# Put-aways of begun products moved behind the second split in the first phase of a two-layer trunk; constants and most parameters loaded in the middle of it

## The chip, the cores and the metric

The kernel runs on one core of one Trainium2 chip. The metric is the device time of one execution in microseconds. The engines are TensorE (PE, matrix products), VectorE (DVE), ScalarE (ACT), GpSimd (POOL) and SyncE (SP, which issues the transfers). Each has a queue of its own that it works off in order; semaphores order the queues among each other.

## The reference, cut to what matters

The program computes two layers on 256 tokens of width 2048 in float32. Layer 0 is a Mamba-2 mixer, layer 1 an attention layer with dilated windows. This case touches the beginning of layer 0:

```python
mod = jax.nn.silu(c) @ w + b                       # per layer: shift, scale, gate
h = x * (1.0 + scale_c) + shift_c
proj = h @ in_w                                    # 2048 x 10304
z, xBC, dt = jnp.split(proj, [SSD_D_INNER, SSD_D_INNER + SSD_CONV_DIM], axis=-1)
xBC = jax.nn.silu(_causal_depthwise_conv(xBC, conv_w, conv_b))
...                                                # scan, gate z, norm, out_w
x = _layer_norm(DEEPNORM_ALPHA * x + (1.0 + gate_c) * y, ln_g[layer], ln_b[layer])
```

## The kernel before

**Products in three passes.** A float32 product is made from halves: `split` copies a raw weight piece (128x1024, 512 KB) to a rounded high half `whi` on ACT (line 93) and computes the low half `wlo` as the difference on DVE (line 95). TensorE then multiplies high by high, high by low and low by high. A *piece* holds two of the 16 tiles `kt` of the contraction (kt = 2q and 2q+1). `cm_piece` (lines 119 to 121) has the weights as the stationary operand and makes 24 matmuls of 256 columns for a piece; `tm_piece` with `tm_mults` (lines 173 to 175) has the activations as the stationary operand and makes 12 matmuls of 512 columns.

**The first phase.** The input `h` is not there at the start: its scale and shift come from `silu(c) @ ada_w`, which DVE computes in 32 dots over 1 MB of `araw` each (`ada_dot`, line 251), two for each kt. Once both dots of a kt are there, `h_step` adds the bias from `adab` (line 256), ACT makes `htmp` and the high half of h (lines 396, 397), and DVE the low half (line 398), which is held back in the list `late` and issued a little later. So kt after kt comes into being while the weights stream in, and TensorE has to work with the few kt that are there. For this the phase does not run one product after the other. Two products (`first`, items -2 and -1, "h" in the list) stay in four PSUM banks of their own for the whole phase. Ten more are *begun*: each takes the pieces whose kt exist already, its sums are then put away to SBUF (`place`), and the rest is added later. The order is written out by hand in `order`, in eight rows of seven pieces with two pieces of `dt` in the last; a dot after the name of a piece ends a stretch of that product. "b4:0." is piece 0 of product b4 and its end for now; "z4:1 z4:2." are pieces 1 and 2 of z4, and there it ends.

**Putting away.** When a stretch ends, the loop issues two instructions for the two PSUM tiles of the product: an ACT copy to `place` (line 486), or, where the product had been put away before, a DVE add (line 484). The other PSUM pool, `mm`, has four buffers, so that two products of the begun kind can be open.

**Transfers.** All loads are issued on SP's queue in program order. `fetch_piece` keeps six raw buffers, `fetch` four araw buffers; an issue waits until its buffer is free, and everything behind it on SP waits too. `prm` holds all small parameters (529 columns: the bias `adab` first with 96, then the convolution's weights and others), `cc` the constants (identity, triangle, mask; 512 columns). Both are loaded in the prologue between the first tiles of x and the first raw pieces.

**Order on an engine.** The program is traced in order, and a planner then sorts the instructions of each engine by its own estimates of when each becomes ready, with the traced order as the priority. `tc.issue_after(ins)` puts the instructions in its block behind `ins` on the queue of the engine of `ins`. The list `pin` holds such an instruction for the dots, `latest` the last low half that `split` issued.

**Behind the phase** come the convolutions of the first two products, the scan and the other products of layer 0, which add their last pieces to the begun sums, and then layer 1.

Of the kernel before, what the change touches and what calls it, by code (L numbers as in the profile page):

```python
# [9 lines left out]
F32 = mybir.dt.float32  # L10
F32R = mybir.dt.float32r
I32 = mybir.dt.int32
AF = mybir.ActivationFunctionType
ALU = mybir.AluOpType
# [4 lines left out]
P = 128  # L19
L = 256  # L20
D = 2048
KT = D // P
# [15 lines left out]
OFF, _o = {}, 0  # L38
# [3 lines left out]
NPAR = _o  # L42
# [7 lines left out]
def trunk(ctx, tc, xT, x, c, par, cst, bias, lnrow, ada, wdt, win, wout, wkv, wk1, wbin, wbout, out):  # L50
    nc = tc.nc
    V, S, T, PO = nc.vector, nc.scalar, nc.tensor, nc.gpsimd

    cons = ctx.enter_context(tc.tile_pool(name="cons", bufs=1))
# [11 lines left out]
    cb_ = cons.tile([P, D], F32, name="cb_")  # L66
    bcast(cb_, c)
    S.activation(cb_, cb_, AF.Silu)
    prm = cons.tile([P, NPAR], F32, name="prm")
    cc = cons.tile([P, NCONST], F32, name="cc")  # L70

    cons.tile([P, 32], F32, name="pad")

    def pv(name):
        a, b = OFF[name]
        return prm[:, a:b]

    ident = cc[:, CI:CI + 128]
    tri = cc[:, CT:CT + 128]
# [5 lines left out]
    def load_piece(src):  # L85
        raw = wp.tile([P, 1024], F32, name="raw", bufs=6)
        nc.sync.dma_start(raw, src)
        return raw

    def split(raw, into=None, after=None):  # L90

        hi, lo = into or [wp.tile([P, 1024], F32R, name=n, bufs=4) for n in ("whi", "wlo")]
        S.activation(hi, raw, AF.Copy)  # L93
        with tc.issue_after(after) if after is not None else ExitStack():
            latest[0] = V.tensor_tensor(lo, raw, hi.bitcast(F32), op=ALU.subtract)  # L95
        return hi.rearrange("p (k n) -> p k n", k=2), lo.rearrange("p (k n) -> p k n", k=2)

    jobs, latest, pin = [], [None], [None]

    def background(n, every=1):  # L100

# [4 lines left out]

    state = [0]

    def cm_piece(src, q, ps, ahi, alo, k0=0, k1=KT, raw=None, after=None):


        hi, lo = split(load_piece(src[q]) if raw is None else raw, after=after)
        for k in range(2):
            kt = 2 * q + k
            for n in range(4):
                o = ps[n // 2][:, n % 2, :]
                c_ = slice(n * P, n * P + P)
                first = kt == k0 and n % 2 == 0
                T.matmul(o, hi[:, k, c_], ahi[:, kt, :], start=first, stop=False, skip_group_check=True)  # L119
                T.matmul(o, hi[:, k, c_], alo[:, kt, :], start=False, stop=False, skip_group_check=True)  # L120
                T.matmul(o, lo[:, k, c_], ahi[:, kt, :], start=False, stop=kt == k1 - 1, skip_group_check=True)  # L121
# [37 lines left out]
    def tiles(ps):  # L159
        return [ps[n // 2][:, n % 2, :] for n in range(4)]  # L160

    def tm_piece(src, q, ps, ahi, alo, k0=0, k1=KT, raw=None):

        tm_mults(q, split(load_piece(src[q]) if raw is None else raw), ps, ahi, alo, k0, k1, range(2))

    def tm_mults(q, w, ps, ahi, alo, k0, k1, blocks, cols=slice(0, 512)):
        hi, lo = (t[:, :, cols] for t in w)
        for k in range(2):
            kt = 2 * q + k
            for b in blocks:  # L170
                h_, l_ = ahi(kt)[:, b * P:b * P + P], alo(kt)[:, b * P:b * P + P]
                o, part = ps[b][:, cols], cols != slice(0, 512)
                T.matmul(o, h_, hi[:, k, :], start=kt == k0, stop=False, skip_group_check=part)  # L173
                T.matmul(o, h_, lo[:, k, :], start=False, stop=False, skip_group_check=part)  # L174
                end = T.matmul(o, l_, hi[:, k, :], start=False, stop=kt == k1 - 1, skip_group_check=part)  # L175
        return end
# [54 lines left out]
    KIND = ("shift", "scale", "gate")  # L231
    mod = [cons.tile([P, KT, 3], F32, name=f"mod{i}") for i in range(2)]
    gated = [dr.tile([D], F32, name=f"gated{i}", bufs=1) for i in range(2)]
    adab = pv("adab").rearrange("p (i k j) -> p i k j", i=2, j=3)

    def shift(i, kt):
        return mod[i][:, kt, 0:1]
# [9 lines left out]
    def ada_dot(layer, kind, ct, raw):  # L247

        j = KIND.index(kind)
        with tc.issue_after(pin[0]) if pin[0] is not None else ExitStack():  # L250
            V.scalar_tensor_tensor(raw, raw, 1.0, cb_, op0=ALU.mult, op1=ALU.mult,  # L251
                                   accum_out=mod[layer][:, ct, j:j + 1])
# [32 lines left out]
    hhi, hlo = hp[:, 0], hp[:, 1]  # L285

    with ExitStack() as cA:
# [14 lines left out]
        with ExitStack() as cS:  # L302
# [21 lines left out]
            def bc_conv(g, t):  # L324
                for i in range(2):
                    bc[g + i] = p0.tile([P, 2, L], F32, name="bcm", bufs=3)
                    conv(t[2 * i], 32 + g + i, bc[g + i][:, 0, :])
                    conv(t[2 * i + 1], 40 + g + i, bc[g + i][:, 1, :])
# [37 lines left out]
            with ExitStack() as c0:  # L366
# [4 lines left out]
                raws, xts, late = [], {}, []  # L371

                def fetch():
                    i = len(raws)
                    if i < len(cols):
                        raws.append(ada_load((wp1, pe)[i // 2 % 2], *cols[i]))
# [5 lines left out]
                def h_step():  # L382

                    _, kind, kt = cols[h_step.i]
                    raw = raws[h_step.i]
                    h_step.i += 1
                    if kind == "scale" and kt % 2 == 0 and kt:
                        fetch_x(kt)
                    ada_dot(0, kind, kt, raw)
                    fetch()  # L390
                    while late:
                        late.pop()()
                    if kind == "shift":
                        ada_bias(0, slice(kt, kt + 1), slice(0, 2))
                        t = pe.tile([P, L], F32, name="htmp")
                        S.activation(t, xts[kt // 2][:, kt % 2, :], AF.Identity, bias=shift(0, kt), scale=scale(0, kt))
                        S.activation(hhi[:, kt, :], t, AF.Copy)
                        late.append(lambda: V.tensor_tensor(hlo[:, kt, :], t, hhi[:, kt, :].bitcast(F32),  # L398
                                                            op=ALU.subtract))
# [4 lines left out]
                part = {n: p[1:] for n, p in zip(names, begun.values())}  # L404
                two = "h"
                order = []
# [11 lines left out]
                source = {"dt": wdt, -2: win[0], -1: win[4], **{n: p[0] for n, p in zip(names, begun.values())}}  # L418
# [3 lines left out]
                def fetch_piece():  # L422
                    if len(pieces) < len(order):
                        k, q, _ = order[len(pieces)]
                        pieces.append(load_piece(source[k][q]))
# [1 line left out]
                fetch()  # L427
                fetch()
                fetch_x(0)
                nc.sync.dma_start(prm, par)  # L430
                nc.sync.dma_start(cc, cst)
                V.tensor_scalar(adab[:, :, :, 1:3], adab[:, :, :, 1:3], 1.0, None, op0=ALU.add)
                fetch_piece()
                fetch_piece()
# [2 lines left out]
                for _ in range(2):  # L437
                    for _ in range(2):
                        h_step()
                    while late:  # L440
                        late.pop()()
                    fetch_piece()

                def dt_piece(q, raw):
# [16 lines left out]
                        T.transpose(pt[:, 64 * b:64 * b + 64], row[:, b * P:b * P + P], ident[:64, :64])  # L461
                    V.tensor_copy(vv, pt)

                begin, done = {}, set()
                for i, (k, q, ends) in enumerate(order):
                    fetch_piece()
                    if k == "dt":
                        dt_piece(q, pieces[i])
                        continue
                    z = str(k)[0] == "z"  # L470
                    if k in part and k not in begin:
                        begin[k] = 2 * q
                        pss[k] = tm_pair() if z else acc_pair()
                    k0, k1 = (begin[k], 2 * q + 2 if ends else KT) if k in part else (0, KT)
                    if z:
                        tm_piece(source[k], q, pss[k], hh_, hl_, k0=k0, k1=k1, raw=pieces[i])
                    else:
                        cm_piece(source[k], q, pss[k], hhi, hlo, k0=k0, k1=k1, raw=pieces[i])
                    if ends:
                        del begin[k]  # L480
                        for w in range(2):
                            place = part[k][1][:, w, :] if z else part[k][1][:, 2 * w:2 * w + 2, :]
                            if k in done:
                                V.tensor_tensor(place, pss[k][w], place, op=ALU.add)
                            else:
                                S.activation(place, pss[k][w], AF.Copy)
                        done.add(k)

                    while h_step.i < min(len(cols), 4 + (i + 1) * 4 // 7):
                        h_step()  # L490
                    while late and h_step.i % 4 == 0:
                        late.pop()()
                bc_conv(0, tiles(first[0]))
                xs_conv(0, tiles(first[1]))
            aux = cS.enter_context(tc.tile_pool(name="aux", bufs=2, space=PSUM, reuse_waits="tile"))
# [533 lines left out]
```

## Time and profile before

| | us |
|---|---|
| median of 3 runs | 1297.56 |
| the runs | 1293.49 to 1298.24 |
| the profiled execution | 1296.34 |
| span in its profile, first to last instruction | 1294.5 |
| mean granted TensorE clock | 0.994 |

The span is cut by lines of the program: `L93` is line 93. A group names engine, operation, output and inputs, count, busy us, mean ns of one, and the idle time in front of its instructions with what ended it. A wait line reads "who waited <- for whom: us in total, times, longest". In a stretch, each engine has its busy time and, in brackets, its number of instructions. PE's ends are modelled, and a matmul counts as busy for longer than until the start of the next, so a PE that shows 10.0 us in 10 can still run at less than its pace. An instruction's idle time stands in square brackets at its end, with what released it.

### The profile page before, as it was taken

The page shows a single profiled execution, that of the slowest core. Times are in us where ns is not written, and L with a number is a line of the kernel's source. Part 1 is how long each engine was busy: PE and PEld are TensorE (multiplying, and loading weights), DVE is VectorE, ACT ScalarE, POOL GpSimd, SP SyncE. Part 2 cuts the span into 40 slices and gives each one's busy share as a digit, 9 for nine tenths or more (in the row PEclk, how much of TensorE's full clock was granted, in tenths as well). Part 3 has the DMA queues.
Part 4 walks back from the last instruction along what each step waited for, and adds up shares of the span by engine and source line. Part 5 has one row for each costly group of instructions (what it writes and reads, how often), then busy time and mean ns, then how long its engine had stood idle before and what let it go on. Part 6 is the DMA issues. An engine that isn't in the chain of part 4 may idle for free.

```text
span 1294.5 us, 19393 instructions
## 1 busy us (share of the span) xinstructions
PE 1247.4 (96%) x7414; PEld 1097.5 (85%) x7414; DVE 1027.1 (79%) x1453; ACT 707.7 (55%) x1033; POOL 27.5 (2%) x20
## 2 busy tenths in 40 slices
PE   4999999999999999999999799999999999999997
PEld 4879988899898999878888699888887888888885
DVE  6789887999999778899765577888777757758778
ACT  3545457867587687864333444444435644444651
POOL 0000000000000000000000043000000000000000
PEclk9999999999999999999999899999999999999999
DMA  9999967696884546398977575999897854363471
GB/s 382 422 398 419 374 210 243 219 342 248 290 313 170 183 161 212 128 338 326 385 258 218 190 238 170 338 393 365 329 342 275 275 187 155 98 187 107 147 276 65
DMA packets 80445, 335.86 MB, mean 259 GB/s; under 512 B 8960, under 2 KB 9056, under 8 KB 67552
## 3 DMA queue, kind: packets, MB, share of 16 engines
q1 hardware_dynamic: 80352, 334.62, 71.5%
q8 instruction: 58, 0.95, 0.3%
q14 instruction: 35, 0.29, 0.1%
HBM read 332.41 MB, written 2.18 MB: 258 GB/s over the span
## 4 chain that ended last, share of the span: by engine, by line
PE 81%; DVE 9%; DMA 5%; ACT 3%; issue 2%; SPq 0%; DVEq 0%; ACTq 0%
PE acc L151 12%; PE acc L174 11%; PE acc L175 11%; PE acc L173 11%; PE acc L121 8%; PE acc L119 8%; PE acc L120 8%; PE acc L152 6%; DMA araw<-in_ada 4%; DVE wlo L95 2%; DVE araw L251 2%; PE py L593 2%; PE aux L802 1%; ACT whi L93 1%; PE po L816 1%
## 5 line engine op out<-in xcount | busy, mean ns | idle before, releaser
L95 DVE TENSOR_TENSOR wlo<-raw,whi 128x1024 fp32r<-128x1024 f32 x395 | 484.4, 1239 | 188.5 <-ACT whi L93 187.5
L93 ACT ACTIVATE whi<-raw 128x1024 fp32r<-128x1024 f32 x395 | 413.0, 1056 | 334.3 <-PE acc L175 139.0
L119 PE MATMUL acc<-actT,whi 128*128 128x256 f32 x960 | 274.1, 289 | 23.2 <-ACT whi L93 19.3
L174 PE MATMUL acc<-wlo,actT 128*128 128x512 f32 x704 | 276.7, 393 | 3.2 <-DVE wlo L95 3.1
L121 PE MATMUL acc<-actT,wlo 128*128 128x256 f32 x960 | 270.8, 286 | 4.4 <-DVE wlo L95 4.4
L173 PE MATMUL acc<-whi,actT 128*128 128x512 f32 x704 | 272.2, 394 | 0.8 <-ACT actT L648 0.7
L120 PE MATMUL acc<-actT,whi 128*128 128x256 f32 x960 | 272.9, 286 | 0.0
L151 PE MATMUL acc<-actT,whi 128*128 128x512 f32 x704 | 251.6, 400 | 0.0
L251 DVE SCALAR_TENSOR_TENSOR araw<-araw,cb__72 128x2048 f32<-128x2048 f32 x96 | 219.3, 2286 | 17.9 <-DMA araw<-in_ada 17.5
L119 PEld LDWEIGHTS acc<-actT,whi 128*128 128x128 f32 x960 | 186.6, 196 | 25.1 <-ACT whi L93 20.3
L152 PE MATMUL acc<-actT,wlo 128*128 128x256 f32 x704 | 201.6, 286 | 0.1
L121 PEld LDWEIGHTS acc<-actT,wlo 128*128 128x128 f32 x960 | 184.6, 194 | 6.7 <-DVE wlo L95 6.4
L120 PEld LDWEIGHTS acc<-actT,whi 128*128 128x128 f32 x960 | 186.7, 194 | 0.4 <-DVE actT L398 0.2
L175 PE MATMUL acc<-whi,actT 128*128 128x512 f32 x448 | 175.0, 391 | 0.0
L174 PEld LDWEIGHTS acc<-wlo,actT 128*128 128x128 f32 x704 | 132.3, 188 | 33.5 <-DVE wlo L95 7.0
L151 PEld LDWEIGHTS acc<-actT,whi 128*128 128x128 f32 x704 | 132.4, 188 | 30.9
L173 PEld LDWEIGHTS acc<-whi,actT 128*128 128x128 f32 x704 | 131.8, 188 | 28.5 <-ACT actT L648 1.5
L152 PEld LDWEIGHTS acc<-actT,wlo 128*128 128x128 f32 x704 | 133.2, 189 | 0.8 <-DVE wlo L95 0.4
L175 PE MATMUL acc<-whi,ylo 128*128 128x512 f32 x256 | 100.3, 392 | 0.0
L175 PEld LDWEIGHTS acc<-whi,actT 128*128 128x128 f32 x448 | 84.1, 188 | 17.1
L175 PEld LDWEIGHTS acc<-whi,ylo 128*128 128x128 f32 x256 | 48.0, 188 | 9.5
L320 DVE SCALAR_TENSOR_TENSOR cacc<-acc,prm,cacc 128x253 f32<-128x253 f32 (+2 forms) x96 | 42.0, 474 | 5.5 <-ACT cacc L317 5.2
(212 smaller groups left out, 1093.0 us busy)
## 6 DMA issues: line engine op xcount, KB each, us to landing
araw<-in_ada SPq DMA_DIRECT2D x96, 1024.0 KB, 7.4
raw<-in_win SPq DMA_DIRECT2D x160, 512.0 KB, 5.3
raw<-in_wkv SPq DMA_DIRECT2D x72, 512.0 KB, 6.2
raw<-in_wout SPq DMA_DIRECT2D x64, 512.0 KB, 4.9
raw<-in_wbin SPq DMA_DIRECT2D x64, 512.0 KB, 4.3
raw<-in_wk SPq DMA_DIRECT2D x24, 512.0 KB, 8.6
cbc<-cumd SPq DMA_DIRECT2D x16, 512.0 KB, 5.4
raw<-in_wbout SPq DMA_DIRECT2D x16, 512.0 KB, 3.7
```

The lines of the kernel that those rows point to most:

```text
L93: S.activation(hi, raw, AF.Copy)
L95: latest[0] = V.tensor_tensor(lo, raw, hi.bitcast(F32), op=ALU.subtract)
L119: T.matmul(o, hi[:, k, c_], ahi[:, kt, :], start=first, stop=False, skip_group_check=True)
L120: T.matmul(o, hi[:, k, c_], alo[:, kt, :], start=False, stop=False, skip_group_check=True)
L121: T.matmul(o, lo[:, k, c_], ahi[:, kt, :], start=False, stop=kt == k1 - 1, skip_group_check=True)
L151: T.matmul(ps[n], hi[:, k, c_], xp[:, kt], start=kt == 0, stop=False, skip_group_check=True)
L152: T.matmul(ps[n][:, 0, :], lo[:, k, c_], xhi[:, kt, :], start=False, stop=kt == KT - 1, skip_group_check=True)
L173: T.matmul(o, h_, hi[:, k, :], start=kt == k0, stop=False, skip_group_check=part)
L174: T.matmul(o, h_, lo[:, k, :], start=False, stop=False, skip_group_check=part)
L175: end = T.matmul(o, l_, hi[:, k, :], start=False, stop=kt == k1 - 1, skip_group_check=part)
L251: V.scalar_tensor_tensor(raw, raw, 1.0, cb_, op0=ALU.mult, op1=ALU.mult, accum_out=mod[layer][:, ct, j:j + 1])
L320: V.scalar_tensor_tensor(acc[:, o:], ps[:, :L - o], w[:, j:j + 1], acc[:, o:], op0=ALU.mult, op1=ALU.add)
```

## The change

The change consists of four edits, all in the first phase.

1. `put_away` replaces the lines that put a begun product's sums away. A stretch that ends with piece i is noted in `ended`, and its put-away is traced in the next turn of the loop, behind the split of piece i+2: copies by `issue_after` behind that piece's ACT copy (`copied`), adds behind its low half (`latest`).
2. For that, each turn traces the split of its own piece (if that is not there yet) and of the next one ahead of the matmuls and of the dots. The pieces' functions get the halves (`w=halves[i]`) instead of the raw piece.
3. `adab` becomes a tile of its own, loaded in the prologue. The rest of `prm` is loaded in the loop at piece 16 and `cc` at piece 20.
4. In the prologue, `pin` is set to the low half of h, so that the dots of kt = 1 and the first of kt = 2 stand behind the low half before them; behind that dot the pin is taken away.

```diff
-    prm = cons.tile([P, NPAR], F32, name="prm")
+    NB = OFF["adab"][1]
+    adab_ = cons.tile([P, NB], F32, name="adab")
+    prm = cons.tile([P, NPAR - NB], F32, name="prm")
...
     def split(raw, into=None, after=None):
         hi, lo = into or [wp.tile([P, 1024], F32R, name=n, bufs=4) for n in ("whi", "wlo")]
-        S.activation(hi, raw, AF.Copy)
+        copied[0] = S.activation(hi, raw, AF.Copy)
...
                     ada_dot(0, kind, kt, raw)
+                    if kt > 1:
+                        pin[0] = None
                     fetch()
...
                 fetch_x(0)
-                nc.sync.dma_start(prm, par)
-                nc.sync.dma_start(cc, cst)
+                nc.sync.dma_start(adab_, par[:, :NB])
...
                     while late:
-                        late.pop()()
+                        pin[0] = late.pop()().ins
                     fetch_piece()
...
+                def put_away(k, ps, add):
+                    for w in range(2):
+                        place = part[k][1][:, w, :] if k[0] == "z" else part[k][1][:, 2 * w:2 * w + 2, :]
+                        with tc.issue_after((latest if add else copied)[0].ins):
+                            if add:
+                                V.tensor_tensor(place, ps[w], place, op=ALU.add)
+                            else:
+                                S.activation(place, ps[w], AF.Copy)
...
                 for i, (k, q, ends) in enumerate(order):
                     fetch_piece()
+                    if i == 16:
+                        nc.sync.dma_start(prm, par[:, NB:])
+                    if i == 20:
+                        nc.sync.dma_start(cc, cst)
+                    for j in (i, i + 1):
+                        if j < len(order) and j not in halves and order[j][0] != "dt":
+                            halves[j] = split(pieces[j])
+                    while ended:
+                        put_away(*ended.pop())
...
                     if ends:
                         del begin[k]
-                        for w in range(2):
-                            place = part[k][1][:, w, :] if z else part[k][1][:, 2 * w:2 * w + 2, :]
-                            if k in done:
-                                V.tensor_tensor(place, pss[k][w], place, op=ALU.add)
-                            else:
-                                S.activation(place, pss[k][w], AF.Copy)
+                        ended.append((k, pss[k], k in done))
                         done.add(k)
...
+                while ended:
+                    put_away(*ended.pop())
                 bc_conv(0, tiles(first[0]))
```

More of the change, by code (lines that the diff above doesn't have):

```diff
@@ L75, in pv @@
         a, b = OFF[name]
-        return prm[:, a:b]
+        return prm[:, a - NB:b - NB]
     ident = cc[:, CI:CI + 128]
@@ L96, in split @@
         return hi.rearrange("p (k n) -> p k n", k=2), lo.rearrange("p (k n) -> p k n", k=2)
-    jobs, latest, pin = [], [None], [None]
+    jobs, latest, copied, pin = [], [None], [None], [None]
     def background(n, every=1):
@@ L107, in trunk, with cm_piece @@
     state = [0]
-    def cm_piece(src, q, ps, ahi, alo, k0=0, k1=KT, raw=None, after=None):
-        hi, lo = split(load_piece(src[q]) if raw is None else raw, after=after)
+    def cm_piece(src, q, ps, ahi, alo, k0=0, k1=KT, w=None, after=None):
+        hi, lo = w or split(load_piece(src[q]), after=after)
         for k in range(2):
@@ L160, in tiles, with tm_piece @@
         return [ps[n // 2][:, n % 2, :] for n in range(4)]
-    def tm_piece(src, q, ps, ahi, alo, k0=0, k1=KT, raw=None):
-        tm_mults(q, split(load_piece(src[q]) if raw is None else raw), ps, ahi, alo, k0, k1, range(2))
+    def tm_piece(src, q, ps, ahi, alo, k0=0, k1=KT, w=None):
+        tm_mults(q, w or split(load_piece(src[q])), ps, ahi, alo, k0, k1, range(2))
     def tm_mults(q, w, ps, ahi, alo, k0, k1, blocks, cols=slice(0, 512)):
@@ L233, in trunk @@
     gated = [dr.tile([D], F32, name=f"gated{i}", bufs=1) for i in range(2)]
-    adab = pv("adab").rearrange("p (i k j) -> p i k j", i=2, j=3)
+    adab = adab_.rearrange("p (i k j) -> p i k j", i=2, j=3)
     def shift(i, kt):
@@ L462, in dt_piece @@
                     V.tensor_copy(vv, pt)
-                begin, done = {}, set()
+                def put_away(k, ps, add):
[6 more added lines that the diff above has]
+                                S.activation(place, ps[w], AF.Copy)
+                begin, done, ended, halves = {}, set(), [], {}
                 for i, (k, q, ends) in enumerate(order):
                     fetch_piece()
+                    if i == 16:
[7 more added lines that the diff above has]
+                        put_away(*ended.pop())
                     if k == "dt":
@@ L475, in trunk @@
                     if z:
-                        tm_piece(source[k], q, pss[k], hh_, hl_, k0=k0, k1=k1, raw=pieces[i])
+                        tm_piece(source[k], q, pss[k], hh_, hl_, k0=k0, k1=k1, w=halves[i])
                     else:
-                        cm_piece(source[k], q, pss[k], hhi, hlo, k0=k0, k1=k1, raw=pieces[i])
+                        cm_piece(source[k], q, pss[k], hhi, hlo, k0=k0, k1=k1, w=halves[i])
                     if ends:
                         del begin[k]
-                        for w in range(2):
-                            place = part[k][1][:, w, :] if z else part[k][1][:, 2 * w:2 * w + 2, :]
-                            if k in done:
-                                V.tensor_tensor(place, pss[k][w], place, op=ALU.add)
-                            else:
-                                S.activation(place, pss[k][w], AF.Copy)
+                        ended.append((k, pss[k], k in done))
                         done.add(k)
```

## The prediction

> **What bounds the kernel now.** First the page: which engine carries the span, and the price of the instructions that the change moves.
>
> ```profile
> span 1294.5 us, 19393 instructions
> ...
> PE 1247.4 (96%) x7414; PEld 1097.5 (85%) x7414; DVE 1027.1 (79%) x1453; ACT 707.7 (55%) x1033; POOL 27.5 (2%) x20
> ...
> L95 DVE TENSOR_TENSOR wlo<-raw,whi 128x1024 fp32r<-128x1024 f32 x395 | 484.4, 1239 | 188.5 <-ACT whi L93 187.5
> L93 ACT ACTIVATE whi<-raw 128x1024 fp32r<-128x1024 f32 x395 | 413.0, 1056 | 334.3 <-PE acc L175 139.0
> ```
>
> TensorE is busy 96% of the span, so the kernel gets faster only by what TensorE stands still, and the change reaches the first phase alone. Second, that phase in stretches (columns: busy us of PE, PEld, DVE, ACT, POOL with instruction counts, granted clock, DMA share, GB/s):
>
> ```profile
> 0.00:20.00 20.00, 4.14 (x17) 3.85 (x18) 9.58 (x12) 6.69 (x7) 0.20 (x4) 1.00 0.90 357
> 20.00:80.00 60.00, 54.58 (x327) 47.99 (x326) 49.10 (x53) 29.21 (x41) 0.00 (x0) 0.97 1.02 422
> 80.00:100.00 20.00, 18.16 (x101) 15.44 (x100) 17.39 (x20) 9.87 (x13) 0.00 (x0) 1.00 0.98 382
> 100.00:140.00 40.00, 40.00 (x279) 37.52 (x278) 34.78 (x37) 21.88 (x28) 0.00 (x0) 1.00 1.01 415
> 140.00:160.00 20.00, 18.34 (x151) 17.93 (x150) 18.90 (x21) 9.62 (x13) 0.00 (x0) 1.00 0.94 364
> 160.00:200.00 40.00, 38.27 (x245) 34.28 (x245) 33.78 (x53) 25.78 (x38) 0.00 (x0) 1.00 0.64 213
> ```
>
> TensorE idles in the start and, in lumps, at 20 to 100 and 140 to 200 us. The DMA engines are full (share 1.02, 422 GB/s) from 20 to 80 us and nearly so to 160: this decides below how much of a gain can stand. Third, the waits from 26 to 200 us, of PE, then of ACT, then of DVE (total us, times, longest):
>
> ```profile
> PE acc L119 <- ACT whi L93: 3.5, 3, 1.6
> PE acc L121 <- DVE wlo L95: 2.7, 5, 1.4
> PE acc L119 <- ACT actT L397: 2.3, 1, 2.3
> PE acc L174 <- DVE wlo L95: 2.1, 3, 1.4
> ...
> ACT y L486 <- PE acc L175: 19.0, 4, 6.4
> ACT sz L486 <- PE acc L175: 8.4, 2, 5.9
> ...
> ACT y L486 <- PE acc L121: 6.3, 4, 3.6
> ...
> ACT whi L93 <- DMA raw<-in_win: 0.2, 1, 0.2
> ...
> DVE y L484 <- PE acc L121: 5.1, 2, 2.8
> ```
>
> PE waits for splits: 3.5 + 2.7 + 2.1 = 8.3 us in 11 stops. ACT and DVE, which make the splits, stand in front of a put-away (L486, L484) until PE ends the product. Fourth, two places in order of time:
>
> ```profile
> 80.91 1.28 ACT L486 ACTIVATE sz<-acc 128x512 f32<-128x512 f32 x2 [5.86 <-PE acc L175]
> 82.08 2.00 ACT L93 ACTIVATE whi<-raw 128x1024 fp32r<-128x1024 f32 x2
> ...
> 83.19 0.39 PE L119 MATMUL acc<-actT,whi 128*128 128x256 f32 x1 [1.63 <-ACT whi L93]
> ...
> 139.61 0.69 DVE L484 TENSOR_TENSOR y<-acc,y 128x512 f32<-128x512 f32 x1 [2.77 <-PE acc L121]
> ...
> 140.94 1.22 DVE L95 TENSOR_TENSOR wlo<-raw,whi 128x1024 fp32r<-128x1024 f32 x1
> ...
> 142.21 0.38 PE L121 MATMUL acc<-actT,wlo 128*128 128x256 f32 x1 [1.44 <-DVE wlo L95]
> ```
>
> At 80.91 ACT has been idle for 5.86 us with a split queued behind the put-away; then come two copies, the split, and only then PE. At 139.61 the same on DVE. The stop has a fixed make-up: the put-away and a split follow the product's end while PE has at most one split piece left.
>
> **The change part by part.**
>
> *Put-aways behind the second split.* No instruction is added: 10 begun products still give 20 copies on ACT and 6 adds on DVE. When a product ends with piece i, ACT now holds the splits of i+1 and i+2 ahead of the copies, so PE has two pieces to eat (24 matmuls at a 0.12 us pitch, about 2.9 us each, 5.7 together) while ACT does 1.28 us of copies and one split of 1.06, and DVE one of 1.24. All 11 stops follow this pattern, so 8.3 us go. Each stop also costs refilling: a 128x512 matmul counts as busy for 0.39 us but the next starts 0.23 later, and the first starts after a stop come about 0.1 late; I take 0.26 per stop, 2.9 us in all (bounds 0 and 11 x 0.4 = 4.4). **Term: 11.2 us, bounds 8.3 and 12.7.**
>
> *What waits behind the put-away now.* On ACT the h pieces (L396, L397) and the split of i+3; these have the 5.7 us. PSUM buffers come free later by at most one split, 1.06 us; this bites only where the next product begins two pieces after an end (x1 after z2, z1 after b2). It is hidden as long as the split of i+2 is done before PE ends piece i; without that cover it costs 1.28 twice. The splits have four buffers of each half; pieces i-1 to i+2 fill them, so a split of i+2 waits at most for PE to leave i-2, which is long past. I take 0 for both.
>
> *Start: prm and cc.* SP's queue, ACT, DVE, and times to landing:
>
> ```profile
> 2.71 0.55 SPq L430 DMA_DIRECT2D prm<-in_par  x1
> 3.29 0.54 SPq L431 DMA_DIRECT2D cc<-in_cst  x1
> ...
> prm<-in_par SPq DMA_DIRECT2D x1, 264.5 KB, 10.1
> cc<-in_cst SPq DMA_DIRECT2D x1, 256.0 KB, 10.2
> ...
> 10.10 2.29 DVE L251 SCALAR_TENSOR_TENSOR araw<-araw,cb__72 128x2048 f32<-128x2048 f32 x1
> ...
> 12.85 0.20 DVE L432 TENSOR_SCALAR prm<-prm 128x64 f32<-128x64 f32 x1 [0.45 <-DMA prm<-in_par]
> ...
> 13.27 0.60 ACT L396 ACTIVATE htmp<-xt,mod 128x256 f32<-128x256 f32 x1 [6.14 <-DVE mod L256]
> 13.90 0.42 ACT L397 ACTIVATE actT<-htmp 128x256 fp32r<-128x256 f32 x1
> 14.71 1.06 ACT L93 ACTIVATE whi<-raw 128x1024 fp32r<-128x1024 f32 x1 [0.39 <-DMA raw<-in_win]
> ...
> 25.72 1.65 PE L119 MATMUL acc<-actT,whi 128*128 128x256 f32 x6 [2.34 <-ACT actT L397]
> ```
>
> prm lands at 2.7 + 10.1 = 12.8 us and cc at 3.3 + 10.2 = 13.5; the loads land one after the other, the first raw piece at 14.7. cc alone took 0.7, prm at most as much as x's tile and it share, about 1.0. The adab tile that stays has 48 of prm's 264.5 KB: 0.2 us by bytes, 1.0 if a DMA's price does not shrink with it. So later loads land 0.7 to 1.5 us earlier; I take 1.2. The first product also needs ACT: the dot ends at 12.4 instead of the wait for prm at 12.85, the h chain moves up 0.6, and the first split then follows it directly at 13.7 instead of 14.71: 1.0. kt = 1, for which PE waits at 25.72, moves by its load, 1.2. **Term: 1.1 us, bounds 0.6 and 1.5.**
>
> The Trainium skill, "DMA: Bandwidth & Descriptors", Specifications, puts line rate at 512 B per transfer and more, and a partition's row of adab is 384 B. By that rule the remaining load is dearer than its bytes, an estimate of 0.4 us instead of 0.2, still inside my bounds; no run here shows such a load.
>
> *Middle: prm and cc again.* The same 1.7 us of transfers less adab now stand at pieces 16 and 20, where the DMA share is 1.02, and two issues of 0.55 us on SP, past which raw and araw issues move. First use of what they carry is behind 150 us. Nothing waits, but every later raw piece lands 1.2 to 1.7 us later than it would; so from there the start's lead on the transfers is spent.
>
> *The pin.* The dot of kt = 2 (2.29 us on DVE) now goes behind the low half of kt = 1. PE stood at most 0.3 us for that half; I take 0.2, inside the start's bounds.
>
> *What is late next.* A PE that runs 8 to 11 us earlier meets pieces that land no earlier. I test it at the tightest place, the piece two behind the put-away at 119.50:
>
> ```profile
> 119.50 1.28 ACT L486 ACTIVATE y<-acc 128x512 f32<-128x512 f32 x2 [6.41 <-PE acc L175]
> ...
> 104.77 4.24 SPq L87 DMA_DIRECT2D raw<-in_win  x2
> ...
> raw<-in_win SPq DMA_DIRECT2D x51, 512.0 KB, 8.4
> ...
> L251 DVE SCALAR_TENSOR_TENSOR araw<-araw,cb__72 128x2048 f32<-128x2048 f32 x25 | 57.1, 2285 | 0.0
> ```
>
> (The last two: the median time to landing until 160 us, and DVE's dots from 30 to 160.) That piece (b4's second after z6) was issued at 104.77 and lands at about 113.2. It needs 1.06 + 1.24 for its split: 115.5. PE wants it at 119.5 + 2.9 = 122.4 now. Of the 8.3 us of idle, 1.66 + 1.73 = 3.4 lie behind 140 us by the stretches, so 4.9 us and seven stops before it: PE will want it 4.9 + 7 x 0.26 + 1.1 + 0.2 = 8.0 us earlier, at 114.4. Missing: 1.1 us, unless transfers come earlier. They can: 80 to 100 us ran at 382 of 422 GB/s, worth 20 x (1 - 382/422) = 1.9 us once buffers come free sooner. So 0.8 us of lead is left, no room for a 2.3 us dot in front of a split on DVE, which is busy 34.78 of 40 us here. Such delays don't add up: once PE has fallen back by one, the lead is there again. From 140 to 160 another 20 x (1 - 364/422) = 2.7 us of transfers can be recovered. **Term: 2.5 us given back, bounds 0 and 6** (6: PE gains only what the transfers gain, see below).
>
> **Sum.** 1.1 + 11.2 + 0.2 - 2.5 = 10.0; the profiled execution took 1296.3 us (span 1294.5), so 1286.3. The median of the runs stands 1.2 above it (1297.56); from the middle of the two, 1297.0, the forecast is **1287.0 us**. Behind 200 us the same work follows, with TensorE full and the DMA share at 0.64, so nothing there should eat the gain; a changed order there I bound by 2 us either way.
>
> **The rivals.**
>
> *All of it holds.* Nothing is given back and the start also keeps its clock. For it: from 100 to 140 us PE ran without a stop against the same transfers. Against: there it had the lead that the change uses up. The granted clock of 0.97 from 20 to 80 us is a half-speed stretch of 0.03 x 60 / 0.5 = 3.6 us, near the wait of 2.34 us at the start; PE loses at most 1.8 us in it, and I take 1.4 because part of it falls on the wait. Time, from the middle of 1297.0 us: 1297.0 - 1.1 - 0.2 - 11.2 - 1.4 = 1283.1.
>
> The Trainium skill, "TensorE: Matmul & The Clock Gate", Why this matters for your kernels, names idle gaps of more than about 3 us as those that halve the clock. The trace does not fit that: the only gap near the half clock is 2.34 us. By the page a gap moved by 1 us stays harmless and the half clock would have no reason to come back; by the trace it comes with such a gap, so this gain stays in the rival.
>
> *The transfers take it back.* The stops turn into waits for raw pieces. For it: share 1.02 from 20 to 80 us, where PE's stops were time in which DMA got ahead. Against: of ACT's waits from 26 to 200 us only 0.2 us are for a raw piece, so the pieces lie landed for a while. Then PE gains only recovered transfer time: 1.9 + 2.7 + 40 x (1 - 415/422) = 0.7, together 5.3, and prm and cc only change place. Time: 1297.0 - 5.3 = 1291.7.
>
> *Slower: the early split blocks DVE.* DVE works in order. A low half of piece i+2 that is queued early waits there for ACT's copy, which waits for the raw piece; behind it stand the dots (2.29 us each, four per seven pieces), whose buffers gate the next araw issues on SP, with the raw issues behind those. By the stretch from 100 to 140, DVE is busy 17.4 us in each 20 that PE takes for seven pieces (four dots and seven splits alone are 4 x 2.29 + 7 x 1.24 = 17.8), so 2.5 us of room. If each of the eight rows of seven pieces loses 3 us beyond that room, 24 us stand against 12.5 gained: 1297.0 + 11.5 = 1308.5. It decides from 1.6 us per row. Against it: DVE already waits for ACT's copies (187.5 us over the whole span) and PE still loses only the 8.3 us here.
>
> **How the numbers follow.** Forecast 0.53 (1284 to 1290.5), all holds 0.16, transfers 0.21, slower 0.10. A measurement of this kernel tells about 0.5%, 6.5 us, from no change. Faster by more than that: forecast and all holds, 0.69; within: transfers, 0.21; slower: 0.10. The range leaves out the slower case and half of the farther ends on both sides: 1281 to 1295.
>
> **What would show it.** First matmul at about 14.8 instead of 15.8; the put-aways on ACT and DVE still wait for PE, but PE's waits for splits from 26 to 200 us fall from 8.3 to under 3 us; the begun products' last adds (198.4 now) come near 188; DMA share near 1 from 80 to 150. Wrong it would be if PE's waits keep their sum with a DMA landing behind them, if dots move late and SP stands before araw, or if the phase ends 10 us earlier and a later stage runs longer.

## The result and the profile after

The changed kernel takes 1286.51 us (median of 4 runs, 1284.66 to 1287.65) where the kernel before took 1297.84 us in the same session. The ratio is 0.9918 with a 95% interval of 0.9897 to 0.9939. The forecast was 1287.0 us. The profiled execution took 1285.96 us, its span is 1284.2 us.

The page of the changed kernel, its two lines that answer to those shown of before:

```profile
span 1284.2 us, 19396 instructions
...
PE 1242.6 (97%) x7414; PEld 1096.4 (85%) x7414; DVE 1027.2 (80%) x1453; ACT 708.5 (55%) x1033; POOL 26.8 (2%) x20
```

The instruction counts of the engines are the same as before; only their order and some loads moved. The same stretches of the first phase (columns as in the prediction):

```profile
0.00:20.00 20.00, 4.85 (x22) 4.50 (x23) 10.37 (x14) 7.04 (x7) 0.20 (x4) 1.00 0.92 365
20.00:80.00 60.00, 55.74 (x363) 50.63 (x362) 54.88 (x59) 34.37 (x49) 0.00 (x0) 1.00 1.02 421
80.00:100.00 20.00, 20.00 (x115) 17.64 (x115) 18.32 (x20) 10.20 (x14) 0.00 (x0) 1.00 1.02 421
100.00:140.00 40.00, 40.00 (x293) 38.11 (x293) 37.86 (x42) 20.38 (x26) 0.00 (x0) 1.00 1.02 423
140.00:160.00 20.00, 20.00 (x158) 19.51 (x157) 19.28 (x21) 10.67 (x15) 0.00 (x0) 1.00 1.00 410
160.00:200.00 40.00, 39.55 (x226) 34.23 (x225) 33.93 (x62) 28.22 (x40) 0.00 (x0) 1.00 0.69 230
```

From 80 to 160 us PE no longer stands still. The DMA share is now 1.00 to 1.02 from 20 to 160 us without the dips at 80 to 100 (0.98 before) and 140 to 160 (0.94 before). And the half clock, 0.97 from 20 to 80 us before, is not in the first phase of this execution. The waits, of PE from 26 to 190 us, and the longest of ACT from 24 to 190 us:

```profile
PE acc L123 <- DVE wlo L97: 1.9, 1, 1.9
...
ACT whi L95 <- DMA raw<-in_win: 46.8, 30, 3.2
```

PE's waits for splits fell from 8.3 us in 11 stops to 1.9 us in one. What ACT waits for has turned round: 33.7 us for the end of a product (19.0 + 8.4 + 6.3) before, now 46.8 us for raw pieces, which before took 0.2. The pieces are split as they land. The prediction had expected the put-aways to go on waiting for PE; ACT's put-aways now wait only 4.8 us for it (2.0 + 1.9 + 0.9), and DVE's not at all.

One put-away on each engine in order of time, ACT's copies and DVE's adds:

```profile
111.29 1.06 ACT L95 ACTIVATE whi<-raw 128x1024 fp32r<-128x1024 f32 x1 [2.58 <-DMA raw<-in_win]
112.26 1.07 ACT L475 ACTIVATE y<-acc 128x512 f32<-128x512 f32 x2
113.21 1.06 ACT L95 ACTIVATE whi<-raw 128x1024 fp32r<-128x1024 f32 x1
...
129.54 2.28 DVE L253 SCALAR_TENSOR_TENSOR araw<-araw,cb__72 128x2048 f32<-128x2048 f32 x1
...
131.75 1.22 DVE L97 TENSOR_TENSOR wlo<-raw,whi 128x1024 fp32r<-128x1024 f32 x1
132.89 1.28 DVE L473 TENSOR_TENSOR y<-acc,y 128x512 f32<-128x512 f32 x2
134.09 1.21 DVE L97 TENSOR_TENSOR wlo<-raw,whi 128x1024 fp32r<-128x1024 f32 x1
```

Neither put-away has idle time in front of it: the split ahead of it ends later than the product, whose last matmul starts at 111.70 and at 131.96 us, so that the put-away finds its sums finished. (Before, the same two stood 6.41 and 2.77 us in front of PE.)

For the experiments I count TensorE's matmul instructions into `acc` from the first one on ("products" below, where they have a number), and give the starts of the 1st, the 100th and the 1100th (the 1100th lies just before the phase ends). The starts come from the profiled execution of each kernel, the time from all its runs. What lies between the last two is the same work in every kernel, except that one of the last experiments moves the pieces of dt forward.

| kernel | 1st | 100th | 1100th | between | time, us |
|---|---|---|---|---|---|
| before | 15.82 | 38.93 | 197.30 | 158.37 | 1297.84 median |
| changed | 15.00 | 35.72 | 184.78 | 149.06 | 1286.51 median |
| constants only | 15.09 | 38.27 | 198.00 | 159.73 | 1297.12 median |
| put-aways only | 15.71 | 36.41 | 185.47 | 149.06 | 1284.73 median |
| one split ahead | 14.92 | 37.02 | 191.89 | 154.87 | 1291.63 median |
| no pin | 15.09 | 34.73 | 183.89 | 149.16 | 1282.62, one run |
| no pin again | 14.99 | 35.80 | 184.87 | 149.07 | 1282.87 median |
| changed again | 14.86 | 35.90 | 184.97 | 149.07 | 1284.02 median |
| three extra loads | 14.93 | 36.91 | 185.97 | 149.06 | 1285.75, one run |
| dots behind | 15.19 | 35.74 | 187.50 | 151.76 | 1293.05, one run |
| six extra loads | 15.14 | 36.02 | 186.70 | 150.68 | 1283.84, one run |

The times come from four sessions. The kernel before had a median of 1298.23 us beside the first four experiments (constants only to no pin), of 1298.91 us beside the next four (no pin again to dots behind), and 1299.47 us in one run beside the six extra loads; ratios are taken within a session.

### The profile page after: what moved, and what is told of

Same layout as the page of the kernel before. It is cut to its first block, busy times and chain, and to the rows that moved or that the text cites. A ratio compares the mean times of both kernels' runs of the same rounds, so it can differ in the third digit from the quotient of the medians.

```text
span 1284.2 us, 19396 instructions
## 1 busy us (share of the span) xinstructions
PE 1242.6 (97%) x7414; PEld 1096.4 (85%) x7414; DVE 1027.2 (80%) x1453; ACT 708.5 (55%) x1033; POOL 26.8 (2%) x20
## 4 chain that ended last, share of the span: by engine, by line
PE 87%; DVE 7%; ACT 3%; DMA 2%; issue 1%; SPq 0%; DVEq 0%; ACTq 0%
PE acc L153 13%; PE acc L176 12%; PE acc L177 12%; PE acc L175 12%; PE acc L121 8%; PE acc L123 8%; PE acc L122 8%; PE acc L154 7%; DMA araw<-in_ada 2%; PE py L612 2%; DVE araw L253 2%; DVE wlo L97 1%; PE aux L821 1%; PE po L835 1%; PE po L845 1%
## 5 line engine op out<-in xcount | busy, mean ns | idle before, releaser
L253 DVE SCALAR_TENSOR_TENSOR araw<-araw,cb__72 128x2048 f32<-128x2048 f32 x96 | 219.2, 2285 | 20.2 <-DMA araw<-in_ada 20.1
```

## The experiments

**Constants only.**

```diff
  kernel before
...
+ adab_ = cons.tile([P, NB], F32, name="adab")      # and prm without it
...
- nc.sync.dma_start(prm, par); nc.sync.dma_start(cc, cst)
+ nc.sync.dma_start(adab_, par[:, :NB])
...
+ if i == 16: nc.sync.dma_start(prm, par[:, NB:])
+ if i == 20: nc.sync.dma_start(cc, cst)
```

> The kernel before with edit 3 alone: adab its own tile, the rest of prm and cc loaded at pieces 16 and 20; put-aways, splits and pin as before. Theory A (the order of put-aways and splits carries the gain): the first matmul comes near 15.0 us instead of 15.8, the first product of dt 1.2 to 3.0 us earlier (before 179.0, after 166.5), PE's waits for splits stay at about 8 us in 11 stops, and the time falls by 1 to 3 us. Rival B (relieving the transfers carries it, put-aways are incidental): dt comes 7 us or more earlier and PE's waits for splits fall under 5 us.

The ratio to before is 0.9991 (0.998 to 1.0003): no gain is shown. The first product came 0.73 us earlier, the 100th 0.66, the 1100th 0.7 later, so the start of dt 1.2 to 3.0 us earlier, which theory A expected, did not come either. PE's waits from 26 to 190 us are those of before:

```profile
PE acc L121 <- ACT whi L95: 3.5, 3, 1.6
PE acc L123 <- DVE wlo L97: 2.8, 5, 1.4
PE acc L176 <- DVE wlo L97: 2.1, 3, 1.4
```

8.4 us of stops are left, so rival B falls: an earlier start alone does not reach the end of the phase. What it had won was lost between 83.9 and 86.9 us, where this execution has a stretch at half clock behind the 1.63 us stop that before has, too. The stretch in the kernel with the constants only:

```profile
80.00:90.00 10.00, 8.17 (x49) 7.41 (x49) 7.40 (x11) 7.24 (x11) 0.00 (x0) 0.83 0.97 358
```

and in the kernel before:

```profile
80.00:90.00 10.00, 8.16 (x57) 7.18 (x56) 7.76 (x10) 6.60 (x10) 0.00 (x0) 1.00 0.98 386
```

**Put-aways only.**

```diff
  kernel changed
- nc.sync.dma_start(adab_, par[:, :NB])             # and the loads at 16 and 20
+ nc.sync.dma_start(prm, par); nc.sync.dma_start(cc, cst)
...
- pin[0] = late.pop()().ins
+ late.pop()()
```

> The kernel changed with prm and cc back in the prologue and without the pin: edits 1 and 2 alone. Theory A: PE's waits for splits fall from 8.3 to 2 or 3 us, dt starts 8.5 to 10 us earlier than before (near 169.5), the time falls by 8 to 10 us. Rival B: dt starts less than 4 us earlier, because pieces land as late as before and the waits only change their name.

The ratio is 0.9891 (0.9872 to 0.991), the whole gain. The first product starts as late as before (15.71), the 1100th 11.8 us earlier, and the work between the 100th and the 1100th takes the 149.06 us of the changed kernel. From 26 to 190 us PE waited for no split at all. The time fell by 13.5 us, more than theory A's 8 to 10 us: in the phase nothing was given back to the transfers. What the time gained beyond the phase's 11.8 us is not explained. Edits 1 and 2 were not parted: the early splits with the put-aways in their old place were not run.

**One split ahead instead of two.**

```diff
  kernel changed
- ended.append((k, pss[k], k in done))
+ put_away(k, pss[k], k in done)                     # behind the split of i+1
```

> The kernel changed, but a put-away stands behind the split of the first piece that follows (i+1) instead of the second; splits are still traced one piece ahead and the constants are as in the change. Theory A: after a product's end PE has 2.9 us of work, the put-away, a copy and a low half take 1.28 + 1.06 + 1.24 = 3.6, so each of some ten ends costs about 0.5 to 1.0 us with refilling: PE's waits for splits come back to 3 to 5 us, dt starts 3 to 6 us later than in the changed kernel (169.5 to 172.5), the time is 3 to 6 us longer than its time. Rival C (tracing the splits early is enough, the second piece is not needed): dt within 1 us of 166.5.

```profile
PE acc L123 <- DVE wlo L97: 4.1, 5, 1.9
PE acc L176 <- DVE wlo L97: 0.7, 2, 0.3
```

PE's waits are 4.8 us, the 1100th product 7.1 us later than in the changed kernel, the ratio to before 0.9944 (0.9928 to 0.996). So rival C falls: the second split is needed. Of the 4.8 us, one stop of 1.87 us at 34.5 us stands in the changed kernel too (1.9 us), so the missing second split accounts for the other 2.9 us: four stops of 0.28 to 0.34 us, and 0.77 and 0.91 us behind two adds. The 7.1 us are more than the 3 to 6 expected: 1.7 us of them are there by 37.9 us, behind a half-clock stretch of 3.4 us that follows the stop at 34.5 us, and the other 5.4 us arise around the six stops, whose 2.9 us therefore cost nearly twice their length.

**No pin.**

```diff
  kernel changed
-                    if kt > 1:
-                        pin[0] = None
...
-                        pin[0] = late.pop()().ins
+                        late.pop()()
```

> The kernel changed without edit 4, the pin on the dots of the prologue. Theory A: worth 0.2 us as predicted, dt starts within 1 us of 166.5. Rival D (the pin carries the earlier start of kt = 1 and with it the full clock there): kt = 1 starts 1 us or more later than 24.3, the half clock is back, dt starts 2 to 4 us later.

The 1100th product is 0.9 us earlier than in the changed kernel, and the stop of 1.9 us at 34.3 us is gone; in its place PE waits 0.5 us at 26.2 us for the low half of kt = 1. Rival D falls for the full clock: it is there without the pin. The reason stands in DVE's order in the changed kernel, with ACT's split and PE's stop:

```profile
28.42 2.28 DVE L253 SCALAR_TENSOR_TENSOR araw<-araw,cb__72 128x2048 f32<-128x2048 f32 x1
...
30.82 2.28 DVE L253 SCALAR_TENSOR_TENSOR araw<-araw,cb__72 128x2048 f32<-128x2048 f32 x1
...
33.03 3.49 DVE L97 TENSOR_TENSOR wlo<-raw,whi 128x1024 fp32r<-128x1024 f32 x3
...
30.55 1.06 ACT L95 ACTIVATE whi<-raw 128x1024 fp32r<-128x1024 f32 x1 [1.84 <-DMA raw<-in_win]
...
34.31 0.39 PE L123 MATMUL acc<-actT,wlo 128*128 128x256 f32 x1 [1.90 <-DVE wlo L97]
```

The copy of the piece is done at 31.6, but a dot of 2.28 us has begun at 30.82, and the low half follows at 33.03.

**No pin once more, and the changed kernel beside it.** The second of these is the changed kernel without an edit.

> The changed kernel without the pin once more, now timed beside the changed kernel (next run). Theory G (the pin puts the dot of 30.8 us ahead of a low half, and PE's stop of 1.9 us at 34.3 us is its price; the earlier kt = 1 is the constants' doing): no stop between 30 and 40 us, dt near 165.6, the time 0.5 to 2 us under that of the changed kernel. Rival D (the pin is worth its place): the time is equal to that of the changed kernel or longer.

> The changed kernel itself, with nothing edited, as the partner of the run before and for the scatter behind the phase. Expected by all: dt within 0.5 us of 166.5, the stop of 1.9 us at 34.3 us there again, the time 9.5 to 12.5 us under that of the kernel before. If the stop of 2.3 us at 555 us and the half clock there come from the change, they are there again; if they are a matter of the single execution, they are not.

Without the pin 1282.87 us (ratio 0.9879, 0.9857 to 0.99), with it 1284.02 us (0.9887, 0.9867 to 0.9907): the intervals overlap, so the pin is not shown to cost or to bring time. The 14.9 us by which the changed kernel beat the kernel before are more than the 9.5 to 12.5 expected here and the 11.3 of the first session. The order on DVE explains the stop. Without the pin a dot stands ahead of the low half of kt = 1 (23.47 and 25.69 us), the later dots come 1.2 us earlier than with it, and the low half of the split follows in time:

```profile
29.59 2.29 DVE L253 SCALAR_TENSOR_TENSOR araw<-araw,cb__72 128x2048 f32<-128x2048 f32 x1
...
31.95 2.48 DVE L97 TENSOR_TENSOR wlo<-raw,whi 128x1024 fp32r<-128x1024 f32 x2
```

PE has no stop between 30 and 40 us, but this execution has the half clock at the start, and the 100th product starts at 35.80 instead of 34.73. Two executions of one program differ by 1.1 us for that alone.

Far behind the phase, near 555 us, the first profile of the changed kernel has a stop of 2.17 us with a half clock of 3.4 us behind it, where the profile of before has a stop of 0.43 us. In the repeat both came again (2.03 us, half clock from 556.2 us). But the stop also stands in the kernel with the constants only, whose first phase is ordered as before, and with 1.79 us in the one with the put-aways only, so it is not the put-aways' doing alone; neither of these two has the half clock there. Why before had 0.43 us stays open, and so does whether the change brings the half clock. The row in order of time, of the constants only:

```profile
568.99 0.44 PE L651 MATMUL aux<-cc,y 128*128 128x128 f32 x2 [2.15 <-DVE ylo L654]
```

and of the changed kernel:

```profile
555.51 0.69 PE L665 MATMUL aux<-cc,y 128*128 128x128 f32 x2 [2.17 <-DVE ylo L668]
```

**Three and six extra loads.** The disputed lead of the transfers, measured by itself.

```diff
  kernel changed
                     if i == 20:
                         nc.sync.dma_start(cc, cst)
+                    if i in (24, 26, 28):             # six: up to 34
+                        nc.sync.dma_start(pe.tile([P, NCONST], F32, ...), cst)
```

> The changed kernel with three more loads of cc's 256 KB each, into tiles of their own, at pieces 24, 26 and 28: 0.79 MB, 1.9 us of transfers at 422 GB/s; nothing waits for them. Theory E (behind the change the pieces are split as they land and PE has about 1 us of lead, so the transfers now set the pace together with PE): PE gets new stops behind piece 28 and dt starts 0.7 to 1.9 us later than 166.5. Rival F (there is lead for more): dt within 0.4 us of 166.5.

The work between the 100th and the 1100th product takes 149.06 us, not 0.1 more than without these loads. PE ran from 80 to 160 us without a stop, and ACT went on waiting for raw pieces. Two stretches, and the wait of ACT from 24 to 190 us, of the kernel with three extra loads:

```profile
80.00:100.00 20.00, 20.00 (x115) 17.64 (x115) 18.90 (x23) 10.70 (x14) 0.00 (x0) 1.00 1.02 422
100.00:140.00 40.00, 40.00 (x293) 38.11 (x292) 37.05 (x41) 18.86 (x24) 0.00 (x0) 1.00 1.02 422
```

```profile
ACT whi L95 <- DMA raw<-in_win: 44.9, 27, 3.2
```

dt starts at 167.7 us, 1.2 us later, which by that number alone would be theory E's; but the lag is there at the 100th product already (a half clock at 24.5 us) and does not grow. So rival F holds in this execution: a full DMA share and splits that wait for their pieces are not yet a limit. The later start helps it, though, since it gives each piece 1.2 us more to arrive. The second kernel asks how far that goes:

> The changed kernel with six extra loads of 256 KB, at pieces 24 to 34, 1.57 MB or 3.8 us of transfers; nothing waits for them. In the changed kernel the low halves of pieces 26 to 37 are ready 1.2 to 2.6 us before TensorE takes them, with three extra loads still 0.8 us. Theory H (the transfers are not the limit of the change, but the lead is some 1.2 to 1.6 us and no more): the lead is used up, PE stops behind piece 32 for 1.5 to 2.6 us in all, and from its hundredth to its eleven hundredth product it takes 150.7 to 151.8 us instead of 149.2. Rival F (buffers refill, any load of this size hides): 149.2 again, within 0.4.

Stretches, and the wait of PE from 26 to 190 us, of the kernel with six:

```profile
100.00:140.00 40.00, 39.41 (x283) 37.10 (x282) 35.39 (x38) 17.49 (x23) 0.00 (x0) 1.00 1.02 421
140.00:160.00 20.00, 19.79 (x154) 19.09 (x153) 19.27 (x22) 11.20 (x14) 0.00 (x0) 1.00 1.02 420
```

```profile
PE acc L123 <- DVE wlo L97: 2.6, 3, 1.9
```

150.68 us, 1.6 more, at the lower end of what theory H expected; two new stops, 0.52 and 0.21 us, stand at 136.8 and 143.0 us, less than its 1.5 to 2.6 us. So of 3.8 us of extra transfers about 2.2 us are free. The lead can also be read directly, as the time from the end of a piece's low half to the first matmul that reads it. For pieces 26 to 37, counted from 0 in the order, it is 1.2 to 2.6 us in the changed kernel. With six loads, at a start only 0.3 us later, it is 0.1 us at piece 35, which stands behind the first three of them: 1.9 us of extra transfers is about what the lead covers. In the profile without the pin, whose TensorE is there about 1 us ahead of the changed kernel's, the lead is already down to 0.1 us at piece 28. So the changed kernel has between 1 and 2 us of lead, read from single executions.

**Dots behind the early split.**

```diff
  kernel changed
                     while h_step.i < min(len(cols), 4 + (i + 1) * 4 // 7):
+                        pin[0] = latest[0].ins
                         h_step()
+                        pin[0] = None
```

> The changed kernel with each dot of the loop put behind the low half of the next piece (i+1) on DVE: the place of the rival that forecast slower. Rival of the prediction (an early low half in front of the dots holds them, their buffers hold SP, the transfers run dry): DMA share falls under 0.95 between 80 and 140 us, PE stops for h or for pieces, dt starts 5 us or more later than 166.5. Theory A (DVE has some 2 us of room in each seven pieces and h is needed late): dt within 1.5 us of 166.5 either way, and the stop at 34.3 us goes, since the dot no longer stands in front of the low half.

The start of dt, at 163.9, is no measure here, as its pieces moved forward in PE's order; the 1100th product is 2.7 us later than in the changed kernel, between the two bounds. The transfers did not run dry (1.02 from 80 to 140 us), so the rival's mechanism does not act in this phase. The stop at 34.3 us is gone, as expected. What ACT waits for is now h, 39.6 us instead of 5.2, and less the raw pieces, 20.2 us instead of 46.8. But the kernel takes 1293.05 us in its one run, 9.0 more than the changed kernel's median in the same session, most of it behind the phase: the stretch from 200 to 240 us of this kernel:

```profile
200.00:240.00 40.00, 35.72 (x228) 31.81 (x227) 25.84 (x40) 26.91 (x45) 0.00 (x0) 0.92 0.62 213
```

and of the changed one:

```profile
200.00:240.00 40.00, 39.57 (x265) 35.94 (x264) 29.78 (x42) 31.86 (x57) 0.00 (x0) 1.00 0.66 231
```

PE stops 4.3 us there, and from 233.8 us the clock falls to half for 10.2 us. The changed order of the convolutions and the scan's first scores is a possible cause; it was not tried by itself.

## Why the prediction was right, and where it was not

**The put-aways** (11.2 us, bounds 8.3 and 12.7). Right in mechanism and size: done alone, they give 197.30 - 185.47 = 11.8 us by the 1100th product, with the half clock at the start in both profiles. 8.3 us of it are the stops of before themselves, so 3.5 us, 0.3 for each stop, are refilling, where the prediction took 0.26. The one-split kernel shows that the second split is what it takes.

**What is late next** (2.5 us given back). This step failed. Nothing was given back: between the 100th and the 1100th product the changed kernel has no stop of PE, and in the execution with 1.9 us of extra loads it takes the same 149.06 us. The prediction worked out a lead of 0.8 us at the tightest piece, from a median time to landing and from PE's need. At that piece, number 33, the profile has the low half done at 113.75 us and PE beginning the piece at 114.80, so 1.0 us: this was about right. What failed is that a dot of 2.3 us in front of a split would use the lead up. Such dots do stand in front of low halves (at 129.54 us in the lines above), but they have mostly run by the time the copy is done: at 131.75 the low half follows its copy by 0.2 us, at 104.50 by 0.8 us, and the lead covers both. That the transfers are near their limit was right, as six loads and the lead of 0.1 us without the pin show; that it already cost was wrong.

**The start** (1.1 us). The first product moved by 0.82 us, kt = 1 from 25.72 to 24.33, so 1.4 instead of 1.2. The load of adab that stays landed 0.3 us behind x's tile (0.4 with the constants only), inside the 0.2 to 1.0 that the prediction allowed. What reaches the 1100th product is 0.6 us (put-aways only against no pin again, both with the half clock), and in time none of it is shown: the constants alone give 0.9991, the put-aways alone as much as the whole. So the size was about right where it arises, half of it reached the end of the phase, and the term is too small to show in the time.

**The pin** (0.2 us). The gain failed. kt = 1's low half did come earlier, which spares PE a stop of 0.5 us, but the reorder put a dot ahead of another low half and PE stood 1.9 us at 34.3 us. Against the kernels without it the changed one is 0.9 us later at the 1100th product where neither has the half clock, and 0.1 us earlier where the other has it. In the time no difference is shown.

**The half clock** was put into the rival "all of it holds". The changed kernel's profile doesn't have it, which with kt = 1 earlier makes z2's first product start at 28.74 instead of 31.71. It isn't shown to be the change's doing: without the pin it is absent in one execution and there in the next, and the changed kernel with three extra loads has it again, although up to there it is the same program. The trace bears out the rule of the Trainium skill that the prediction cited ("TensorE: Matmul & The Clock Gate", Why this matters for your kernels, gaps of more than about 3 us) only in part: half clocks of 6.8 to 10.2 us came with the one stop over 3 us behind the start (5.7 us, near 730 us) in all eleven profiles, but half clocks followed stops of 1.63 and 1.87 us too.

**Behind the phase** (2 us either way). The profiled execution is 12.5 us ahead at the 1100th product and 10.4 us at the end; the repeat, which ran in another session, 12.3 and 11.8. The loss stands at one place: across the stop and the half clock near 555 us the lead over before falls from 12.5 to 9.8 us. Taken from kernel to kernel (before, put-aways only, no pin again, no pin, changed), the 12.5 us part into 11.8 for the put-aways, 0.6 for the constants, 1.0 for the half clock that is absent, and -0.9 for the pin. So that the forecast hit 1287 within 0.5 us is partly luck, errors that cancel: nothing was given back (2.5 us better than the sum) and the half clock was absent (1.0 better), but the pin's stop (1.1 worse) and the loss behind the phase (2.1 worse) took that back. In mechanism the rival "all of it holds" describes the phase better than the forecast, and the repeat, 1284.02 us, lies near its 1283.1.

The slower rival: DVE did not come to hold the transfers, not even with all dots behind the early splits. The rival that the transfers take it back is excluded for this change: between the 100th and the 1100th product PE does not stop, and 12.5 us reached the end of the phase where the rival left 5.3.

No version is clearly faster than the changed kernel. The one without the pin, 1282.87 us, is as fast with one edit less, and the put-aways with the early splits alone, 1284.73 us, with two edits less.

## What to carry to other kernels

When a sum that must be put away stands in an in-order queue ahead of the work that feeds TensorE, count how long TensorE can live on what is ready, and put as many feeding steps ahead of the put-away as that takes: here two, as one brought back 2.9 us of waits in six stops. A full DMA share and an engine that waits for each load don't prove that loads are the limit; add loads that nobody needs and see when the end moves, and compare only with a profile whose start is as early. And look at the whole order after an edit that pins one instruction: the cost came two splits later on the same queue.

## What was not expected of the hardware

The granted clock fell to half behind stops of only 1.63 us (constants only, at 83 us) and 1.87 us (one split ahead, at 34.5 us), while the same stops in other executions passed without it (before at 83 us; the changed kernel at 34.3 us). An estimate from its length, 3.4 us at half pace, is up to 1.7 us of difference between executions of the same order; without the pin 1.1 us were measured. And TensorE's pace without stops is very even: 149.06 to 149.16 us for the same 1000 products in six executions of four kernels.
